# Layer-0 conditioning sums on ScalarE and GpSimd in place of TensorE matvecs

## The chip, the cores and the metric

The kernel runs on one core of one Trainium2 chip. Its time is the device time of one execution in microseconds; the time of a kernel is the median of its runs. All times below are of this metric or of one profiled execution of the kernel before.

## What is computed

The reference is a decoder trunk of two layers over 256 tokens of width 1024, in float32. A vector `c` of 1024 conditions each layer:

```python
c_act = jax.nn.silu(c)
for l in range(DEPTH):
    mod = c_act @ ada_w[l] + ada_b[l]
    sh_m, sc_m, g_m, sh_f, sc_f, g_f = jnp.split(mod, 6, axis=-1)
    h = modulate(rms_norm(x, norm_mix_g[l]), sh_m, sc_m)
    proj = h @ w_in[l]
    ...
    mixed = jnp.concatenate([attn_out, ssm_out], axis=-1) @ w_out[l]
    x = x + g_m[:, None, :] * mixed
    h = modulate(rms_norm(x, norm_ffn_g[l]), sh_f, sc_f)
    ...
    x = x + g_f[:, None, :] * f
```

The mixer between `proj` and `mixed` is a sliding-window attention beside a state-space mixer; `f` is a dense SwiGLU in layer 0 and a top-2-of-8 mixture of experts in layer 1. Each of the six parts of `mod` is a product of a vector of 1024 and a matrix of 1024 x 1024. The change is about two of them in layer 0: the mixer's gate `g_m` and the feed-forward shift `sh_f`.

## The kernel before

All weights come in one fixed order through a stream of 8 raw buffers of 128 x 2080 floats (`Stream`, loads at line 124 on SyncE's queue). A unit is one load of about 1 MB. A buffer is given back when its unit has been read, and the next load in the order waits for a free buffer. Weights for matmuls are split first: ScalarE copies a tile of 128x1024 into a rounded format (`hi`, line 157), VectorE subtracts that from the raw tile (`lo`, line 158), and each product is three matmuls (lines 698 to 700). Splits run about two half units ahead of their use. Conditioning units (kind `raw`) are used as they come, unsplit.

Layer 0 runs so: the first two parts of `mod`; the input projections (features bc and x, then q, kv, z0, z1 in `tok_tile`); beside them the chains of the mixer, small generators that `tick()` advances between matmuls; then `out_proj`, four steps in the order `WO_ORDER`, each with one unit of output weights; then the norm, the modulation, and the dense feed-forward (`ffn`). The framework's scheduler orders the instructions of each engine in advance by a priority that follows the order of tracing; an instruction whose inputs are ready may be moved ahead of one that waits. On the chip each engine then goes through its queue in order.

The parts are numbered relative to the fourth: part -2 is `g_m`, part -1 is `sh_f`, part 0 is `sc_f`, part 1 is `g_f`. Each has four units (`k2` = 0 to 3) of 256 rows of `ada_w`. Parts -2, -1 and 0 are matvecs on TensorE in `ada_half`: for each unit the matmuls at line 610 multiply the column of `c_act`, spread over 32 columns, with the loaded tile, and four column groups add up in one PSUM bank `ps("a")`, of which there is one. After the last unit ScalarE copies the bank (line 615), four transposes (line 618) turn it into columns in the same bank, and VectorE adds the bias (lines 622, 623). The units of part -2 lie among the input projections, one each after x1, q0, q1 and kv (`FILL`, run by `fill()`); those of parts -1 and 0 lie behind the output weights in the stream and behind `out_proj` in the program. Part 1 is not a matvec: `half_late` scales and adds on VectorE into an accumulator and then sums over the partitions with matmuls against ones (line 580).

`g_m` is first needed at the residual update in the last step of `out_proj` (line 1179), `sh_f` and `sc_f` at the modulation after the norm (`make_amp`, `modulate`). GpSimd has little to do: the products of the decay with the state-space scores at line 1043 and one product at line 1060, in each layer, and a few in the router.

Of the kernel before, what the change touches and what calls it, by code (L numbers as in the profile page):

```python
# [7 lines left out]
F32 = mybir.dt.float32  # L8
# [3 lines left out]
AF = mybir.ActivationFunctionType  # L12
OP = mybir.AluOpType
AX = mybir.AxisListType

P = 128
D = 1024
# [202 lines left out]
def trunk(ctx, tc, x, c, positions, ada_w, ada_b, norm_mix_g, norm_ffn_g, w_in, w_out, attn_sinks,  # L220
# [3 lines left out]
    V, A, G, PE = nc.vector, nc.scalar, nc.gpsimd, nc.tensor  # L224
# [4 lines left out]
    act = ctx.enter_context(tc.tile_pool(name="act", bufs=1))  # L229
    psum = ctx.enter_context(tc.tile_pool(name="psum", bufs=1, space=bass.MemoryType.PSUM))  # L230

    def ps(tag):
        return psum.tile([P, 512], F32, name="ps_" + tag, tag=tag, bufs={"w": 3, "m": 3, "d": 1, "a": 1}[tag])
# [6 lines left out]
    def add_w(tag, loads, n):  # L240
        units.append(dict(kind="w", tag=tag, loads=loads, n=n))
# [6 lines left out]
    def add_rows(tag, w2d, r0, nrow):  # L248
        src = w2d[r0:r0 + nrow * P, :].rearrange("(k p) f -> p k f", p=P)
        add_w(tag, [(0, nrow * D, src)], nrow * D)  # L250
# [38 lines left out]
    def add_ada_half(l, part, k2):  # L289
        src = ada_w[l, k2 * 2 * P:(k2 + 1) * 2 * P, 4096 + part * D:4096 + (part + 1) * D].rearrange("(k p) f -> p k f", p=P)  # L290
        units.append(dict(kind="raw", tag=("adah", l, part, k2), n=2048, loads=[(0, 2048, src)]))

    WO_ORDER = (2, 3, 0, 1)

    def wo_units(l):
        for kp in WO_ORDER:
            add_rows(("wo", l), w_out[l], kp * 256, 2)

    def add_first(half, k2):
        rows = ada_w[0, k2 * 2 * P:(k2 + 1) * 2 * P, :]  # L300
        units.append(dict(kind="raw", tag=("first", half, k2), n=2048, loads=[
            (i * D, (i + 1) * D, rows[:, i * D + half * 512:i * D + half * 512 + 512].rearrange("(k p) f -> p k f", p=P))
            for i in range(2)]))

    for k2 in range(4):
        add_first(0, k2)
    FILL = (0, 0, 0, 1, 1, 1, 1, 0, 0)
    n = 0
    win0 = win_units(0)
    for i, j in enumerate(FIRST):  # L310
        win0[j]()
        for k2 in FIRST_FILL.get(i, ()):
            add_first(1, k2)
        for _ in range(FILL[i]):
            add_ada_half(0, -2, n)
            n += 1
    assert n == 4
    wo_units(0)
    for part in (-1, 0):
        for k2 in range(4):  # L320
            add_ada_half(0, part, k2)
    n_ffn = 3 * FFN // 256
    n_late = 3 * KT + 4
    ada_at = [n_late * min(i + 1, LATE_FFN) // LATE_FFN - n_late * min(i, LATE_FFN) // LATE_FFN for i in range(n_ffn)]
    n = 0
# [54 lines left out]
    S = Stream(nc, raw_pool, split_pool, units)  # L380
# [5 lines left out]
    ident = const.tile([P, P], F32)  # L386
# [22 lines left out]
    ones = const.tile([P, P], F32)  # L409
# [21 lines left out]
    ct = const.tile([P, KT], F32)  # L431
    p = ps("w")
# [29 lines left out]
    for b in range(2):  # L462
        for h in range(2):
            p = ps("w")
# [5 lines left out]
    adab = const.tile([P, 96], F32)  # L470
# [47 lines left out]
    modT = [const.tile([P, 48], F32, name=f"modT{l}") for l in range(DEPTH)]  # L518
# [82 lines left out]
    def ada_half(l, part, k2):  # L601
        j, t = S.take_raw(("adah", l, part, k2))
        if k2 == 0:
            ada_ps[0] = ps("a")
        p = ada_ps[0]
        for k in range(2):
            kk = k2 * 2 + k
            for i in range(2):
                q = k * 2 + i
                PE.matmul(p[32 * q:32 * q + 32, :], ct[:, kk:kk + 1].to_broadcast([P, 32]),  # L610
                          t[:, k * D + i * 512:k * D + (i + 1) * 512], start=(k2 == 0), stop=(k2 == 3))
        S.release(j)
        if k2 == 3:
            r = act.tile([P, D], F32, name="adar", tag="adar")[:, 0:512]
            A.activation(r, p, AF.Copy)
            p2 = ps("a")
            for i in range(4):
                PE.transpose(p2[:, i * P:(i + 1) * P], r[:, i * P:(i + 1) * P], ident)
            pv = p2.rearrange("p (j c) -> p c j", j=4)[:, 0:P:32, :]
            o0 = 32 + part * 8  # L620
            dst = modT[l][:, o0:o0 + 8].rearrange("p (c j) -> p c j", c=2)
            V.tensor_tensor(dst, pv[:, 0:2, :], adab[:, l * 48 + o0:l * 48 + o0 + 8].rearrange("p (c j) -> p c j", c=2), op=OP.add)
            V.tensor_tensor(dst, pv[:, 2:4, :], dst, op=OP.add)

    def mod(l, i):
        return modT[l][:, i * 8:(i + 1) * 8]
# [98 lines left out]
    def fill():  # L725
        if filler:
            for f in filler.pop(0):
                f()
# [58 lines left out]
    def mixer(l, h, second=None, third=None):  # L787
# [20 lines left out]
        cbm = cx[:, 0].rearrange("p (i t) -> p i t", i=4)  # L808
# [153 lines left out]
        def wait_for(*keys):  # L962
            while not all(k in ready for k in keys):
                yield 1

        def dt_chain(bx):
# [33 lines left out]
            for ch in range(2):  # L1000
                for g in range(2):
                    spawn(decay(ch, g))
                    yield DEC_Y
# [20 lines left out]
        def decay(ch, g):  # L1024
            bc = ps("m")
            PE.matmul(bc, identb, dmask4.rearrange("p a b -> p (a b)"), start=True, stop=False, skip_group_check=True)
            for h4 in range(4):
                hh = ch * 8 + g * 4 + h4
                PE.matmul(bc[:, h4 * P:(h4 + 1) * P], dta[:, hh:hh + 1].to_broadcast([P, P]), tri, start=False, stop=True,
                          skip_group_check=True)  # L1030
            yield 1
            mt = act.tile([P, 4, P], F32, name="mt", tag="mt" if ch == 0 else "sm", bufs=2 if ch == 0 else 4)
            mts[ch, g] = mt
            for h4 in range(4):
                hh = ch * 8 + g * 4 + h4
                A.activation(mt[:, h4, :], bc[:, h4 * P:(h4 + 1) * P], AF.Exp, bias=nacs[:, hh:hh + 1])
            if ch == 0:
                ec = eac[:, g * 4:g * 4 + 4]
                V.tensor_tensor(ec, bc.rearrange("p (h t) -> p h t", h=4)[:, :, P - 1], acs[:, g * 4:g * 4 + 4], op=OP.subtract)
                A.activation(ec, ec, AF.Exp)  # L1040
            yield from wait_for("cbm")
            yield 1
            G.tensor_tensor(mt, mt, cbm[:, ch * 2 + g, :][:, None, :].to_broadcast([P, 4, P]), op=OP.mult)
            ready.add(("decay", ch, g))

        def x_chain(b0, b1):
# [109 lines left out]
    def out_proj(l, m, norm, route=None):  # L1156
        mhi, mlo, ready = m
        banks = [ps("w"), ps("w"), ps("w"), ps("d")]
        for n, kp in enumerate(WO_ORDER):
            while (("mix", kp) if kp < 2 else ("ssm", kp - 2)) not in ready:  # L1160
                tick()
            if l == 1 and n == 0:
                assert {"y", "k", "qt"} <= ready
                S.lend(first_moe + LIMIT, lambda: [act.tile([P, D], F32, name="slot", tag=t) for t in ("cx", "qr")])
            w = S.take(("wo", l), 2)
            if n == 3 and route:
                route.prepare()
                S.lend(first_moe + LATE_LIMIT, lambda: [act.tile([P, D], F32, name="slot", tag=t) for t in ("misc", "adar")])
                S.lend(first_moe + LIMIT, lambda: [act.tile([P, 2 * D], F32, name="slot", tag="xbc")])
                S.lend(first_moe + SM_LIMIT, lambda: [act.tile([P, 512], F32, name="slot", tag="sm", bufs=4) for _ in range(4)])  # L1170
            for k in range(2):
                kk_ = 2 * kp + k
                last = n == 3 and k == 1
                for m_ in range(8):
                    b = banks[m_ // 2][:, (m_ % 2) * T:(m_ % 2 + 1) * T]
                    mm3(b, w.hi(k, m_ * P, (m_ + 1) * P), w.lo(k, m_ * P, (m_ + 1) * P), mhi[:, kk_, :], mlo[:, kk_, :],
                        n == 0 and k == 0 and m_ % 2 == 0, last)
                    if last:
                        V.scalar_tensor_tensor(xT[:, m_, :], b, mod(l, 2)[:, m_:m_ + 1], xT[:, m_, :], op0=OP.mult, op1=OP.add)
                        norm.add(m_)  # L1180
                        if route:
                            route.add(m_)
                    if m_ == 3:
                        tick()
                S.used()
                tick()
        assert not chains
# [579 lines left out]
        modulate_part(rbc, 0, 0, amps[0], h, range(4, KT))  # L1767


    steps = [lambda k2=k2: ada_half(0, -2, k2) for k2 in range(4)]  # L1770
    for n in FILL:
        filler.append(steps[:n])
        steps = steps[n:]
    m = mixer(0, h, second, third)
    norm = Norm()
    out_proj(0, m, norm)
    for part in (-1, 0):
        for k2 in range(4):
            ada_half(0, part, k2)
    amp = make_amp(0, 1)  # L1780
    h = modulate(norm, 0, 1, amp)
    dn = ffn(h, [lambda k2=k2: half_late(0, 1, k2) for k2 in range(4)] +
# [42 lines left out]
```

## Time and profile before

| what | value |
|---|---|
| median of 3 runs | 1399.41 us (1398.51 to 1399.52) |
| profiled execution, own time | 1397.93 us |
| its span, first to last instruction | 1395.8 us |
| TensorE busy | 1321.7 us (95%) |
| VectorE busy | 857.9 us (61%) |
| ScalarE busy | 643.7 us (46%) |
| GpSimd busy | 20.1 us (1%), 22 instructions |
| mean granted TensorE clock | 0.98 |

The busy shares are of the whole span, over stages with different limits. PE is TensorE's matmuls, PEld its weight loads, DVE VectorE, ACT ScalarE, POOL GpSimd, SP SyncE. The end of a matmul is modelled, so distances from start to start say more than its duration. In rows of a timeline, the bracket at the end is the idle time of the engine before the instruction and what ended it.

### The profile page before, as it was taken

To read this page: it belongs to the slowest core of one execution; us is meant where nothing else is said; L and a number is where in the kernel's file an instruction comes from. 1 tells how busy PE (TensorE), PEld (TensorE's weight loads), DVE (VectorE), ACT (ScalarE), POOL (GpSimd) and SP (SyncE) were. 2 spreads that over 40 slices of the span, in tenths; PEclk is the share of its full clock that TensorE was granted. 3 is DMA by queue.
4 is the path that set the end of the run, shared out by engine and by line. 5 is a ranking of instruction groups with operands and counts; after the bars stand their busy time and mean duration, and the time that the engine had idled before them with its cause. 6 is when DMAs were issued, how large, how long until landed. Compare 5 with 4: busy or idle time off the path is not lost. (4 is left out here: it accounts for less than half of the span.)

```text
span 1395.8 us, 20220 instructions
## 1 busy us (share of the span) xinstructions
PE 1321.7 (95%) x7642; PEld 953.8 (68%) x7642; DVE 857.9 (61%) x1297; ACT 643.7 (46%) x923; POOL 20.1 (1%) x22
## 2 busy tenths in 40 slices
PE   6999999999899979999999999987999999999996
PEld 3788699999798868666464756656557467756643
DVE  5587598778689579556254744546537348845532
ACT  3456454444465547445143543533536236744412
POOL 0020000000020010000000000000000000000000
PEclk9999999999999989999999999997999999999998
DMA  9963799999434549899999999989999999999993
GB/s 324 349 237 109 277 388 363 325 348 340 159 127 146 197 149 340 333 406 400 402 409 409 409 409 409 398 349 400 363 409 409 402 401 409 409 379 409 402 402 127
DMA packets 158214, 468.77 MB, mean 336 GB/s; under 512 B 10560, under 2 KB 39456, under 8 KB 155040
## 3 DMA queue, kind: packets, MB, share of 16 engines
q1 hardware_dynamic: 155616, 466.72, 87.8%
q8 instruction: 61, 1.00, 0.3%
q10 hardware_dynamic: 2496, 0.72, 0.2%
q14 instruction: 41, 0.34, 0.1%
HBM read 466.36 MB, written 1.05 MB: 335 GB/s over the span
## 5 line engine op out<-in xcount | busy, mean ns | idle before, releaser
L158 DVE TENSOR_TENSOR lo<-raw,hi 128x1024 fp32r<-128x1024 f32 (+1 forms) x346 | 413.4, 1226 | 98.5 <-ACT hi L157 95.3
L157 ACT ACTIVATE hi<-raw 128x1024 fp32r<-128x1024 f32 (+1 forms) x346 | 354.9, 1057 | 220.7 <-PE ps_m L699 69.2
L699 PE MATMUL ps_w<-lo,xh 128*128 128x512 f32 x352 | 141.1, 401 | 0.7 <-DVE lo L158 0.7
L700 PE MATMUL ps_w<-hi,xh 128*128 128x512 f32 x352 | 140.3, 400 | 0.2 <-DVE xh L1503 0.2
L698 PE MATMUL ps_w<-hi,xh 128*128 128x512 f32 x352 | 133.8, 404 | 6.9 <-PEq L1246 5.6
L158 DVE TENSOR_TENSOR lo<-slot,hi 128x1024 fp32r<-128x1024 f32 (+1 forms) x112 | 128.0, 1181 | 15.7 <-ACT hi L157 15.7
L157 ACT ACTIVATE hi<-slot 128x1024 fp32r<-128x1024 f32 (+1 forms) x112 | 111.6, 1026 | 33.2 <-PE ps_w L700 25.7
L1673 DVE TENSOR_TENSOR sg<-sg,ps_w 128x512 f32<-128x512 f32 (+1 forms) x32 | 20.9, 654 | 171.6 <-PE ps_w L1524 129.8
L1524 PE MATMUL ps_w<-raw,xl 128*64 128x512 f32 (+1 forms) x624 | 125.7, 545 | 0.0
L698 PE MATMUL ps_m<-act_hi,hi 128*128 128x256 f32 (+1 forms) x368 | 104.6, 285 | 7.6 <-ACT hi L157 4.7
L700 PE MATMUL ps_m<-act_hi,lo 128*128 128x256 f32 (+1 forms) x368 | 104.1, 284 | 0.4 <-DVE lo L158 0.4
L699 PE MATMUL ps_m<-act_lo,hi 128*128 128x256 f32 (+1 forms) x368 | 104.2, 284 | 0.0
L1524 PEld LDWEIGHTS ps_w<-raw,xl 128*64 128x64 f32 x624 | 43.9, 137 | 72.2 <-issue 65.7
L1580 ACT ACTIVATE hh<-ps_m 128x512 fp32r<-128x512 f32 x28 | 16.2, 595 | 154.9 <-PE ps_m L1575 131.8
L698 PEld LDWEIGHTS ps_w<-hi,xh 128*128 128x128 f32 x352 | 67.3, 192 | 23.5 <-issue 5.9
L1524 PE MATMUL ps_w<-slot,xl 128*64 128x512 f32 (+1 forms) x400 | 81.4, 536 | 0.0
L699 PEld LDWEIGHTS ps_w<-lo,xh 128*128 128x128 f32 x352 | 67.4, 191 | 17.7 <-DVE lo L158 1.9
L700 PEld LDWEIGHTS ps_w<-hi,xh 128*128 128x128 f32 x352 | 67.0, 191 | 16.4 <-DVE xh L1503 0.7
L1546 PE MATMUL ps_m<-raw,ht 128*64 128x512 f32 x328 | 76.6, 599 | 0.0
L698 PEld LDWEIGHTS ps_m<-act_hi,hi 128*128 128x128 f32 (+1 forms) x368 | 68.1, 185 | 11.5 <-ACT hi L157 5.2
L1582 DVE TENSOR_TENSOR hl<-ps_m,hh 128x512 fp32r<-128x512 f32 x28 | 18.8, 688 | 92.8 <-ACT hh L1580 92.8
L1672 ACT ACTIVATE sg<-ps_w 128x512 f32<-128x512 f32 (+1 forms) x44 | 24.9, 576 | 102.5 <-PE ps_w L1524 76.6
(428 smaller groups left out, 2484.3 us busy)
## 6 DMA issues: line engine op xcount, KB each, us to landing
raw<-in_moe_w_down SPq DMA_DIRECT2D x84, 1024.0 KB, 13.5
raw<-in_moe_w_gate SPq DMA_DIRECT2D x79, 1024.0 KB, 12.4
raw<-in_moe_w_up SPq DMA_DIRECT2D x61, 1024.0 KB, 12.6
raw<-in_ada_w SPq DMA_DIRECT2D x40, 1024.0 KB, 7.2
slot<-in_moe_w_up SPq DMA_DIRECT2D x25, 1024.0 KB, 14.0
slot<-in_moe_w_gate SPq DMA_DIRECT2D x48, 512.0 KB, 12.7
slot<-in_moe_w_up SPq DMA_DIRECT2D x46, 512.0 KB, 13.8
slot<-in_moe_w_down SPq DMA_DIRECT2D x20, 1024.0 KB, 13.7
```

What stands on the lines that cost most here:

```text
L157: self.last_hi = nc.scalar.activation(hi[:, o:o + w], t, AF.Copy).ins
L158: self.last_lo = nc.vector.tensor_tensor(lo[:, o:o + w], t, hi[:, o:o + w].bitcast(F32), op=OP.subtract).ins
L698: PE.matmul(o_, s_hi, m_hi, start=start, stop=False, skip_group_check=True)
L699: PE.matmul(o_, s_hi, m_lo, start=False, stop=False, skip_group_check=True)
L700: PE.matmul(o_, s_lo, m_hi, start=False, stop=stop, skip_group_check=True)
L1524: PE.matmul(b[half * c_:half * (c_ + 1), 0:wide], xl[:, kk_, :], S.col(j, o_, o_ + wide), start=(kk_ == 0), stop=(kk_ == KT - 1), skip_gro ...
L1546: PE.matmul(y[half * c_:half * (c_ + 1), :], ht[:, ft % nm, ft // nm, :], S.col(j, t_ * D + c_ * 512, t_ * D + (c_ + 1) * 512), start=(ch ...
L1580: A.activation(hh, pv, AF.Copy)
L1582: V.tensor_tensor(hl, pv, hh.bitcast(F32), op=OP.subtract)
L1672: A.activation(s_[:, 0:wide], g_[:, 0:wide], AF.Silu)
L1673: V.tensor_tensor(s_[:, 0:wide], s_[:, 0:wide], u_[:, 0:wide], op=OP.mult)
```

## The change

The matvecs of parts -2 and -1 go. In their place, `slow_half` scales each loaded tile of 128x1024 in its buffer on ScalarE by the matching value of `c_act`, and GpSimd adds the tiles up in the buffer of the part's first unit, which is held until the part is done. The sums after the first product at line 1043 are put behind the latest one that has been traced (`mixed_by`). `slow_out` then adds over the partitions with matmuls against ones, as `half_late` does, and transposes as before. The units come in another order: two units of part -2 after x1 and two after z0, two of part -1 after z1 and one each with the first two output weights. `slow_out` of part -2 stands ahead of the third step of `out_proj`, that of part -1 behind `out_proj`. Part 0 stays a matvec.

```diff
-    FILL = (0, 0, 0, 1, 1, 1, 1, 0, 0)
+    FILL = (0, 0, 0, 2, 0, 0, 0, 2, 2)
+    SLOW = [(part, k2) for part in (-2, -1) for k2 in range(4)]
...
         for _ in range(FILL[i]):
-            add_ada_half(0, -2, n)
+            add_ada_half(0, *SLOW[n])
             n += 1
-    assert n == 4
-    wo_units(0)
-    for part in (-1, 0):
-        for k2 in range(4):
-            add_ada_half(0, part, k2)
+    for i, kp in enumerate(WO_ORDER):
+        add_rows(("wo", 0), w_out[0], kp * 256, 2)
+        if i < 2:
+            add_ada_half(0, *SLOW[n])
+            n += 1
+    assert n == len(SLOW)
+    for k2 in range(4):
+        add_ada_half(0, 0, k2)
...
+    slow_acc = {}
+    mixed_by = []
+
+    def slow_half(l, part, k2):
+        j, t = S.take_raw(("adah", l, part, k2))
+        if k2 == 0:
+            slow_acc[part] = j, t[:, 0:D]
+            A.activation(t[:, 0:D], t[:, 0:D], AF.Copy, scale=ct[:, 0:1])
+        acc = slow_acc[part][1]
+        for k in range(2):
+            kk = k2 * 2 + k
+            if kk:
+                tk = t[:, k * D:(k + 1) * D]
+                A.activation(tk, tk, AF.Copy, scale=ct[:, kk:kk + 1])
+                with ExitStack() as after:
+                    if mixed_by:
+                        after.enter_context(tc.issue_after(mixed_by[-1]))
+                    G.tensor_tensor(acc, acc, tk, op=OP.add)
+        if k2:
+            S.release(j)
+
+    def slow_out(l, part):
+        j, acc = slow_acc.pop(part)
+        p = ps("a")
+        for i in range(2):
+            PE.matmul(p[32 * i:32 * i + 32, :], ones[:, 0:32], acc[:, i * 512:(i + 1) * 512], start=True, stop=True)
+        r = act.tile([P, D], F32, name="adar", tag="adar")
+        A.activation(r[0:64, 0:512], p[0:64, :], AF.Copy)
+        S.release(j)
+        p2 = ps("a")
+        for i in range(4):
+            PE.transpose(p2[:, i * P:i * P + 64], r[0:64, i * P:(i + 1) * P], ident[0:64, 0:64])
...
-            G.tensor_tensor(mt, mt, cbm[:, ch * 2 + g, :][:, None, :].to_broadcast([P, 4, P]), op=OP.mult)
+            mult = G.tensor_tensor(mt, mt, cbm[:, ch * 2 + g, :][:, None, :].to_broadcast([P, 4, P]), op=OP.mult)
+            mixed_by.append(mult.ins)
...
             w = S.take(("wo", l), 2)
+            fill()
+            if l == 0 and n == 2:
+                slow_out(0, -2)
...
-    steps = [lambda k2=k2: ada_half(0, -2, k2) for k2 in range(4)]
-    for n in FILL:
+    steps = [lambda s=s: slow_half(0, *s) for s in SLOW]
+    for n in FILL + (1, 1):
         filler.append(steps[:n])
         steps = steps[n:]
...
     out_proj(0, m, norm)
-    for part in (-1, 0):
-        for k2 in range(4):
-            ada_half(0, part, k2)
+    slow_out(0, -1)
+    for k2 in range(4):
+        ada_half(0, 0, k2)
```

## Rows read from the trace of the kernel before

**Rows 1.** Windows: busy us (instructions) per engine, granted clock, DMA share, GB/s.
```profile
60.00:140.00 80.00, 78.35 (x601) 65.32 (x599) 66.09 (x174) 50.40 (x126) 8.00 (x5) 1.00 0.53 182
166.90:170.50 3.60, 3.55 (x15) 3.25 (x16) 3.60 (x10) 2.08 (x5) 0.00 (x0) 0.54 1.05 403
220.00:260.00 40.00, 40.00 (x338) 39.02 (x337) 31.78 (x26) 17.04 (x20) 0.00 (x0) 1.00 0.99 351
```
**Rows 2.** Timeline of TensorE, layer 0's mixer: start us, us, line, operation.
```profile
66.06 0.50 PE L698 MATMUL ps_w<-hi,act_hi 128*128 128x512 f32 x1
...
95.81 0.63 PE L922 MATMUL ps_m<-ident,qr 128*128 128x128 f32 x4 [0.53 <-DVE qr L829]
96.36 1.06 PE L610 MATMUL ps_a<-raw,ct 128*32 128x512 f32 x8
97.36 0.39 PE L698 MATMUL ps_w<-hi,act_hi 128*128 128x256 f32 x1
...
116.02 0.39 PE L698 MATMUL ps_w<-mx_hi,hi 128*128 128x256 f32 x1
```
**Rows 3.** Timeline of TensorE, layer 1's mixer.
```profile
397.78 1.05 PE L1012 MATMUL ps_m<-xbc 128*128 128x128 f32 x8
...
400.30 0.39 PE L698 MATMUL ps_w<-hi,act_hi 128*128 128x512 f32 x1
...
444.63 0.38 PE L698 MATMUL ps_w<-mx_hi,hi 128*128 128x256 f32 x1
```
**Rows 4.** Timeline of TensorE, from layer 0's norm to the feed-forward.
```profile
159.27 0.50 PE L665 MATMUL ps_m<-sel,npart 128*128 128x1 f32 x4
160.14 3.64 PE L610 MATMUL ps_a<-raw,ct 128*32 128x512 f32 x32 [0.37 <-PE ps_m L665]
...
164.55 0.66 PE L618 MATMUL ps_a<-ident,adar 128*128 128x128 f32 x4
166.93 0.40 PE L698 MATMUL ps_m<-act_hi,hi 128*128 128x256 f32 x1 [1.72 <-ACT act_hi L692]
```
**Rows 5.** Timeline of TensorE, from layer 1's first norm to its projections.
```profile
366.25 0.61 PE L665 MATMUL ps_m<-sel,npart 128*128 128x1 f32 x4 [0.47 <-ACT npart L662]
...
371.66 0.38 PE L698 MATMUL ps_m<-act_hi,hi 128*8 128x256 f32 x1 [1.18 <-ACT act_hi L692]
```
**Rows 6.** Timeline of TensorE, column sum of `half_late`.
```profile
197.46 1.05 PE L580 MATMUL ps_a<-adacc,ones 128*32 128x512 f32 x4
```
**Rows 7.** Groups by line, ScalarE, 60 to 140: count, busy us, mean ns, idle before.
```profile
L157 ACT ACTIVATE hi<-raw 128x1024 fp32r<-128x1024 f32 x18 | 19.1, 1065 | 10.2 <-PE ps_w L700 9.8 <-PE ps_d L699 0.4
```
**Rows 8.** Timeline of GpSimd, layer 0's mixer.
```profile
80.97 1.28 POOL L1043 TENSOR_TENSOR mt<-mt,cx 128x512 f32<-128x512 f32 x1 [79.26 <-ACT mt L1036]
83.03 3.51 POOL L1043 TENSOR_TENSOR mt<-mt,cx 128x512 f32<-128x512 f32 x2 [0.79 <-ACT mt L1036]
86.51 1.04 POOL L1060 TENSOR_TENSOR cx<-xx,eac 128x512 f32<-128x512 f32 x1
87.51 2.27 POOL L1043 TENSOR_TENSOR mt<-mt,cx 128x512 f32<-128x512 f32 x1
```
**Rows 9.** One line's instructions, L1404 on GpSimd: ns min/median/max.
```profile
L1404 POOL TENSOR_TENSOR htok_l<-ht,htok_h x3: 1277/1317/1318, 497.1 to 501.4; 128x512 fp32r<-128x512 f32 x3
```
**Rows 10.** Timeline of VectorE, splits beside GpSimd's products, both layers.
```profile
83.22 2.18 DVE L158 TENSOR_TENSOR lo<-raw,hi 128x1024 fp32r<-128x1024 f32 x1
...
86.66 1.98 DVE L158 TENSOR_TENSOR lo<-raw,hi 128x1024 fp32r<-128x1024 f32 x1
...
416.42 1.48 DVE L158 TENSOR_TENSOR lo<-raw,hi 128x1024 fp32r<-128x1024 f32 x1 [0.53 <-ACT hi L157]
```
**Rows 11.** One line's instructions, L158 (60 to 140) and L829: ns min/median/max.
```profile
L158 DVE TENSOR_TENSOR lo<-raw,hi x18: 1208/1218/2176, 60.6 to 135.1; 128x1024 fp32r<-128x1024 f32 x18
...
L829 DVE TENSOR_TENSOR qr<-rm,rm x4: 679/684/1775, 88.6 to 428.3; 128x512 f32<-128x512 f32 x4
```
**Rows 12.** Timeline of SyncE's queue, loads of parts -1 and 0.
```profile
85.97 50.72 SPq L124 DMA_DIRECT2D raw<-in_ada_w  x8
```

More of the change, by code (lines that the diff above doesn't have):

```diff
@@ L623, in ada_half @@
             V.tensor_tensor(dst, pv[:, 2:4, :], dst, op=OP.add)
+    slow_acc = {}
[28 more added lines that the diff above has]
+            PE.transpose(p2[:, i * P:i * P + 64], r[0:64, i * P:(i + 1) * P], ident[0:64, 0:64])
+        pv = p2.rearrange("p (j c) -> p c j", j=4)[:, 0:64:32, :]
+        o0 = 32 + part * 8
+        V.tensor_tensor(modT[l][:, o0:o0 + 8].rearrange("p (c j) -> p c j", c=2), pv,
+                        adab[:, l * 48 + o0:l * 48 + o0 + 8].rearrange("p (c j) -> p c j", c=2), op=OP.add)
     def mod(l, i):
```

## The prediction

> **What bounds the kernel now.** I read the windows first, to find out what sets the pace where the change acts and whether a shift there survives to the end. In the feed-forward stage TensorE is busy for all 40.00 us of 220 to 260 at full clock, with VectorE at 31.8 and ScalarE at 17.0 [rows 1]. Nothing there can take up a microsecond that is won or lost earlier, and the later stages start from TensorE's progress, so I carry every shift to the end one for one. In layer 0's mixer, from 60 to 140, TensorE is busy for 78.35 of 80 us, but VectorE is busy for 66.09 too and ScalarE for 50.40, while GpSimd has only 8.00 [rows 1]. So this stretch has two engines near their limit, and the question of the whole case is which of the two a microsecond is taken from.
>
> Then TensorE's timeline. One half of a matvec part is 8 matmuls of 128x512 and pushes the next projection matmul back by 1.00 us (96.36 to 97.36) [rows 2]. Layer 1 runs the same mixer without any such matvecs and is the best witness for what taking them out can give. From its first q matmul to its first output-projection matmul it needs 444.63 - 400.30 = 44.33 us, and 1.0 us of small matmuls (line 1012) that layer 0 has inside its stretch lie ahead of it in layer 1: 45.3 us [rows 3]. Layer 0 needs 116.02 - 66.06 = 49.96 us [rows 2]. That is 4.6 us more, of which three halves are 3.0.
>
> After the output projection the chain runs through the norm: from the matmul at line 665 over the reciprocal root on VectorE to the first feed-forward matmul. It takes 166.93 - 159.27 = 7.66 us [rows 4]. Between the two stand 32 matvec matmuls of part 0 (3.64 us from 160.14): they could not start earlier, because part -1 held the single bank `ps_a`, and the amplitude waits for their transposes at 164.55 [rows 4]. The same chain in front of layer 1, with no matvecs, takes 371.66 - 366.25 = 5.41 us [rows 5].
>
> **The change part by part: TensorE.** It loses 8 halves of 1.00 us, 8.0 us in all, and gains two column sums of four matmuls, 1.05 us each by the like sum of the feed-forward shift [rows 6], 2.1 us. The transposes stay. Net that is 5.9 us less work. What reaches the end is asked place by place.
>
> Part -2 lies in the mixer. Layer 1 says that up to 4.6 us can go, if VectorE keeps up; at worst nothing goes, if VectorE sets the pace. I take the four halves, 4.0 us. Its sum moves ahead of the third step of the output projection, where TensorE runs dense: +1.05 us. Together -2.95 (from -4.6 to +1.05).
>
> Part -1 lies around the output projection and in front of the norm. Its sum can now be made during the output projection, so `ps_a` comes free earlier and part 0's matmuls, which stay, go into the places that part -1's had; the reciprocal root is then left alone. The difference between the two chains, 7.66 - 5.41 = 2.25, is the upper bound; nothing is the lower one, if the sums are late. I take -2.0, near layer 1, as its chain is the same code.
>
> **ScalarE** gets 16 scalings of 128x1024. The nearest row is the split's copy of the same size, 1,065 ns [rows 7]: 17 us, against 29.6 us that ScalarE is idle from 60 to 140 [rows 1]. They stand in order among the copies and exponentials that feed VectorE and TensorE. Free would be 0; if one of six delays a waiting unit by its length, about 3. I take +1.0, and the idle time is the cover: without it all 17 would be on the path.
>
> **GpSimd** gets 14 sums of 128x1024, all with both inputs in SBUF. None is in the trace. A sum of half the size takes 1.04 us at least (line 1060, with one input broadcast) [rows 8] and 1.317 with two full inputs (line 1404) [rows 9]. Doubled, this gives 2.1 to 2.6 us; I take 2.5, near the full inputs, so 35 us (29 to 37). GpSimd has the time. VectorE hasn't: when GpSimd works on SBUF, a VectorE instruction with two SBUF inputs stands still. The split at line 158 takes 1.21 us at its least, and 2.18 and 1.98 beside GpSimd's products; line 829 takes 0.68 and once 1.77 [rows 8, 10, 11]. In turn the products at 83.03 and 87.51 stretch (3.51 for two, 2.27 for one, against 1.28 alone): the two engines take turns [rows 8]. So layer 0's five GpSimd instructions, 4 x 1.28 + 1.04 = 6.2 us of work, cost VectorE 0.97 + 0.77 + 1.09 = 2.8 us, a share of 0.46. In layer 1 the same five cost only 1.48 - 1.21 = 0.27 [rows 10, 11], a share of 0.04. These are my bounds, 1.5 to 17 us. I take 0.4, so 14 us: the new sums stand in layer 0, they are twice as long, so that a VectorE instruction that meets one waits longer, and VectorE splits a weight tile there 18 times in 80 us [rows 11].
>
> How much of the 14 reaches TensorE? VectorE is idle for 80 - 66.09 = 13.9 us in the stretch [rows 1], so at best nothing; at worst all of it. After the 2.8 us above, TensorE waited for VectorE only 0.53 us (line 922 at 95.81) [rows 2], a share of 0.19: one short burst fits into the lead that the splits have. A burden that lasts through the whole attention doesn't, because that idle time is largely time in which VectorE waits for products of the other engines, and it moves along when they are late. I let 5 of the 14 be absorbed: +9.0 (from 0 to +17).
>
> A sentence of the Trainium skill gives another price: "GPSIMD Engine Reference", section 3.1, measures a GpSimd add of 2,048 elements at 4,497 ns, so half of it, 2.25 us, is an estimate for one sum here. By that page 14 sums take 31.5 us, 12.6 of them as VectorE's waiting and 7.6 on the path, and the total below would be 1.4 us lower. The trace has no sum of this length. The same page's section 4.1 advises VectorE for elementwise work, since GpSimd is about half as fast; no row here weighs that for this size.
>
> **Loads.** The eight units of parts -2 and -1 are issued among the projections' and output weights, and SyncE's queue is passed in order. Before, the last 8 conditioning loads trickle out for 50.72 us from 85.97, because no buffer is free [rows 12]. Afterwards two of eight buffers stay held, each until its sum is read, but the other six are released before the norm. The queue is slack, so I price this at 0; it would cost if an output weight came behind a unit that GpSimd holds.
>
> **Sum** against the profiled execution, 1397.93 us (span 1395.8): -2.95 - 2.0 + 1.0 + 9.0 = +5.05, so 1402.98. The median of the runs is 1.48 above the profiled execution: 1404.5.
>
> **Rivals.**
> (a) GpSimd's sums fall between VectorE's two-input work as in layer 1, a share of 0.04. Then VectorE loses 1.5 us, all absorbed, the scalings cost nothing, and -4.95 is left: 1394.5 as a median; with layer 1's full 4.6 and 2.25, 1393.6 (-6.85 + 1.05). For it: VectorE is idle for 13.9 us of the stretch, and what it does otherwise than with two SBUF inputs isn't held up; against it: layer 0 has shown 0.46. It decides as soon as less than 2.2 us of waiting reaches TensorE. Chance 0.25.
> (b) The two cancel: a share of 0.19 of the 14 us reaches TensorE as at 95.81, 2.7 us, with +1.0 for ScalarE: -1.3, so 1398.2. Chance 0.20.
> (c) GpSimd falls behind: the 11 sums behind the products (the last of which starts at 87.51) run from about 90; if each takes 2.5 us and waits for two splits of 1.21, they end at 144, and with late scalings near 157, when part -1's sum is due for the norm. From there on it decides: the tail gains nothing (+2.0) and the first feed-forward matmul waits for sum, transposes and shift, some 3 us more by the 2.4 us from 164.55 to 166.93: +10, so 1409.5. Against it: their units are loaded early. Chance 0.10.
> (d) The forecast. Chance 0.45.
>
> The waits have a second price. After TensorE stood still for 1.72 us before 166.93, the granted clock was 0.54 from 166.9 to 170.5, its lower level, 1.2 GHz instead of 2.4 [rows 1, 4]; that cost some 1.7 us. One or two more such stops are the upper part of my range.
>
> **Numbers.** About 0.2%, 2.8 us, is what a measurement tells from no change. Faster: (a), 0.25. Same: (b), 0.20. Slower: (c) and (d), 0.55. The forecast's own range is 1401 to 1412 (2.7 more or less of the waiting hidden; a stop of the clock or two more). The range for 8 in 10 takes in (a): 1393 to 1413.
>
> **What would show it.** Right: GpSimd busy some 35 us more; in layer 0's mixer splits of about 2 us where 1.2 is clean, VectorE's busy time 10 us or more above 66; the first output-projection matmul later than 116.02; line 665 to the first feed-forward matmul in 5.4 us. Wrong: splits that stay at 1.2 us beside the sums, or line 698 after the mixer at 112, would give rival (a). What would make me wrong most easily is the order: sums that run while VectorE evicts PSUM.

## The result and the profile after

The changed kernel takes 1416.50 us (median of 5 runs, 1413.38 to 1416.97) against 1398.94 us for the kernel before (median of 5 runs beside it): a ratio of 1.0118 (95% interval 1.0107 to 1.013), 17.6 us slower by the medians. The sign of the forecast holds, its size doesn't: +5.05 was forecast, and the time lies above the range. The profiled execution took 1414.5 us with a span of 1412.7 us, 16.9 more than the span before.

The windows come first, as before the change (columns as in [rows 1]).
```profile
60.00:140.00 80.00, 65.75 (x429) 57.71 (x429) 76.55 (x153) 52.39 (x106) 45.07 (x19) 0.89 0.55 189
180.00:190.00 10.00, 8.88 (x50) 8.56 (x50) 6.31 (x16) 4.46 (x9) 0.00 (x0) 0.66 0.79 291
220.00:260.00 40.00, 40.00 (x341) 40.00 (x340) 32.04 (x25) 17.39 (x19) 0.00 (x0) 1.00 1.02 373
```
In the mixer TensorE is busy for 65.75 of 80 us where it was 78.35, and VectorE for 76.55 where it was 66.09, with fewer instructions (153 for 174). So VectorE now sets the pace. The granted clock fell from 1.00 to 0.89. The feed-forward stage is as dense as before.

TensorE's timeline shows where the time goes; it answers to [rows 2 to 5].
```profile
64.53 0.80 PE L739 MATMUL ps_w<-hi,act_hi 128*128 128x512 f32 x2 [0.22 <-DVE xbc L991]
...
97.95 1.09 PE L963 MATMUL ps_m<-ident,qr 128*128 128x128 f32 x4 [3.73 <-DVE qr L870]
109.22 0.47 PE L884 MATMUL ps_m<-ident,kr 128*128 128x128 f32 x1 [2.96 <-DVE kr L872]
127.41 1.09 PE L1148 MATMUL ps_m<-ident,zy 128*128 128x128 f32 x4 [5.50 <-DVE zy L1142]
...
131.29 0.58 PE L739 MATMUL ps_w<-mx_hi,hi 128*128 128x256 f32 x1
...
172.43 1.47 PE L614 MATMUL ps_a<-raw,ct 128*32 128x512 f32 x9
...
176.72 0.60 PE L706 MATMUL ps_m<-sel,npart 128*128 128x1 f32 x4
...
181.62 0.58 PE L739 MATMUL ps_m<-act_hi,hi 128*128 128x256 f32 x1 [1.12 <-ACT act_hi L733]
```
The first q matmul is 1.53 us earlier (66.06 to 64.53). The first output-projection matmul is 15.27 later (116.02 to 131.29): nearly the whole loss arises between these two. Three waits for VectorE, 12.2 us in all, stand there, where before there was one of 0.53 [rows 2]. The first feed-forward matmul is 14.69 later (166.93 to 181.62), and the end 16.9 later; the clock of 0.66 from 180 to 190, behind the stops at the norm, lies in the last step.

GpSimd's timeline answers to [rows 8].
```profile
57.91 7.35 POOL L646 TENSOR_TENSOR raw<-raw 128x1024 f32<-128x1024 f32 x3 [56.20 <-ACT raw L642]
82.39 1.31 POOL L1084 TENSOR_TENSOR mt<-mt,cx 128x512 f32<-128x512 f32 x1 [17.13 <-ACT mt L1077]
...
91.60 32.07 POOL L646 TENSOR_TENSOR raw<-raw 128x1024 f32<-128x1024 f32 x11
```
Eleven sums run back to back from 91.60 to 123.67, a mean of 2.9 us each. In the same stretch VectorE's timeline reads:
```profile
92.87 2.18 DVE L158 TENSOR_TENSOR lo<-raw,hi 128x1024 fp32r<-128x1024 f32 x1
94.98 2.82 DVE L870 TENSOR_TENSOR qr<-rm,rm 128x512 f32<-128x512 f32 x1
...
101.03 2.44 DVE L872 TENSOR_TENSOR kr<-rm,rm 128x128 f32<-128x128 f32 x1
103.40 3.40 DVE L158 TENSOR_TENSOR lo<-raw,hi 128x1024 fp32r<-128x1024 f32 x1
...
116.04 2.08 DVE L1134 TENSOR_TENSOR zy<-zy 128x512 f32<-128x512 f32 x1
118.05 3.42 DVE L158 TENSOR_TENSOR lo<-raw,hi 128x1024 fp32r<-128x1024 f32 x1
121.39 1.27 DVE L918 TENSOR_REDUCE st<-ps_m 128x2 f32<-128x512 f32 x2
122.59 1.10 DVE L675 TENSOR_SCALAR rs_v<-gs 128x2 f32<-128x2 f32 x1
```
Splits of 1.21 us take up to 3.42, and line 870 takes 2.82 where 0.68 is clean [rows 11]. This instruction makes the `qr` that TensorE waited 3.73 us for. Line 918, which reads PSUM, is not stretched. I added up, over all VectorE instructions from 45 to 200 us, what each took beyond the shortest of its line and operands in any of the traces: 5.6 us before, 24.9 after. This sum is called the excess below.

One line's instructions (ns min/median/max), splits first:
```profile
L158 DVE TENSOR_TENSOR lo<-raw,hi x16: 1214/1440/3424, 64.7 to 137.4; 128x1024 fp32r<-128x1024 f32 x16
...
L642 ACT ACTIVATE raw<-raw,ct x14: 1135/1142/1270, 56.7 to 118.6; 128x1024 f32<-128x1024 f32 x14
```

### The profile page after: what moved, and what is told of

It reads as the page before. It is cut to its first block, busy times and chain, and to the rows that moved or that the text cites. A ratio compares the mean times of both kernels' runs of the same rounds, so it can differ in the third digit from the quotient of the medians.

```text
span 1412.7 us, 20171 instructions
## 1 busy us (share of the span) xinstructions
PE 1324.0 (94%) x7586; PEld 959.4 (68%) x7586; DVE 876.6 (62%) x1295; ACT 659.3 (47%) x939; POOL 59.2 (4%) x36
## 3 DMA queue, kind: packets, MB, share of 16 engines
HBM read 466.36 MB, written 1.05 MB: 331 GB/s over the span
## 5 line engine op out<-in xcount | busy, mean ns | idle before, releaser
L158 DVE TENSOR_TENSOR lo<-raw,hi 128x1024 fp32r<-128x1024 f32 (+1 forms) x346 | 422.3, 1253 | 99.2 <-ACT hi L157 97.5
L158 DVE TENSOR_TENSOR lo<-slot,hi 128x1024 fp32r<-128x1024 f32 (+1 forms) x112 | 128.2, 1184 | 15.6 <-ACT hi L157 15.4
L741 PEld LDWEIGHTS ps_w<-hi,xh 128*128 128x128 f32 x352 | 67.2, 191 | 16.4 <-DVE xh L1548 0.7
```

Of the source, the lines that this page charges most:

```text
L158: self.last_lo = nc.vector.tensor_tensor(lo[:, o:o + w], t, hi[:, o:o + w].bitcast(F32), op=OP.subtract).ins
L741: PE.matmul(o_, s_lo, m_hi, start=False, stop=stop, skip_group_check=True)
```

## The experiments

The theory: GpSimd's sums hold VectorE up, and TensorE waits for VectorE. The rivals: ScalarE's scalings in the order of its queue, the new order of the loads, and GpSimd being late with its own work and with the buffers. Each ratio is to runs of the kernel before on the same chip.

**No sums.**
```diff
-                    G.tensor_tensor(acc, acc, tk, op=OP.add)
```


> The changed kernel without GpSimd's 14 sums; ScalarE's 16 scalings, the order of the loads and both column sums stay (the sums themselves are left out, so each part keeps only its first scaled row block). Theory (the sums keep VectorE's two-input instructions waiting, and that is the loss): VectorE's splits are back at 1.2 us, first output-projection matmul at 113 to 117 us instead of 131.29, and the time falls from 1416.5 to 1393 to 1399 us. Rival, ScalarE's 17 us of scalings in the order of its queue are the loss: still above 1408 us. Rival, the new order of the loads is the loss: still above 1408 us, though buffers come free sooner here.

1398.80 us, ratio 1.0000 (0.9991 to 1.0009). The splits of this run, by one line's instructions:
```profile
L158 DVE TENSOR_TENSOR lo<-raw,hi x19: 1207/1219/2295, 64.2 to 136.8; 128x1024 fp32r<-128x1024 f32 x19
```
Median 1,219 ns again, and the output projection starts at 116.23. Neither scalings nor order are the loss: without the sums the time is that of the kernel before. But nothing is gained either: the 4 us that the removed matvecs were to bring are missing, which two runs below follow up.

**No scalings.**
```diff
-                A.activation(tk, tk, AF.Copy, scale=ct[:, kk:kk + 1])
```


> The changed kernel without ScalarE's 16 scalings; GpSimd sums the tiles as loaded (the factors of c are left out). Theory: the 14 sums stay, so the time stays at 1412 to 1417 us; the scalings are worth 0 to 3 us. Sums that needn't wait for a scaling can start earlier, so the stretch of long VectorE instructions moves forward. Rival, ScalarE's scalings are the loss: 1405 us or less.

1416.22 us, 1.0125 (1.011 to 1.0141): the loss without any scaling. The splits' median is 2.06 us here:
```profile
L158 DVE TENSOR_TENSOR lo<-raw,hi x15: 1210/2059/3425, 68.1 to 137.5; 128x1024 fp32r<-128x1024 f32 x15
```

**The order alone.** All eight halves by `ada_half`, at the changed kernel's places; no `slow_out`.
```diff
-    steps = [lambda s=s: slow_half(0, *s) for s in SLOW]
+    steps = [lambda s=s: ada_half(0, *s) for s in SLOW]
```


> TensorE's matvecs as before, but at the places and in the order of loads of the changed kernel: both parts' eight halves in the input-projection's slots and ahead of the first two output-projection steps, no scaling, no sum, no column sum. Theory: the order alone costs nothing; part -1's four halves leave the stretch behind the last output-projection step (-0.6 to -2.8 us by the two traces) and go into stretches in which TensorE partly waits, so 1395 to 1400 us. Rival, the order of the loads (input and output projection weights held up behind the eight halves) is the loss: above 1408 us.

1402.41 us, 1.0025 (1.0016 to 1.0034): 3.3 us slower, above what the theory gave and far below its rival. The first output-projection matmul is 5.73 us later than before, as part -1's matvecs now stand in the mixer, and only 1.5 come back by the first feed-forward matmul.

**Writing in place of summing.** One write of zeros for each sum, then three.
```diff
-                    G.tensor_tensor(acc, acc, tk, op=OP.add)
+                    for _ in range(3):   # or once
+                        G.memset(tk, 0.0)
```


> In place of each of the 14 sums GpSimd writes zeros over the scaled tile (128x1024, nothing read), at the same place in its queue, with the same waits, and the buffers are released behind it (the sums are left out). Theory (a GpSimd instruction that reads holds up VectorE's two-input instructions): splits of 1.2 us, 1393 to 1400 us, even if GpSimd is busy for 20 us or more with the writing. Rival, what GpSimd's queue delays (its own products behind the sums, the buffers that it releases late): if one write takes over 2 us the time stays above 1408 us. Rival, any GpSimd instruction on the memory holds VectorE up: above 1405 us, with splits of 2 us.

> Three writes of zeros in place of each of the 14 sums (42 instructions that read nothing, at 0.95 us as the run with one write showed, so about 40 us of GpSimd instead of the sums' 36 us), with the same waits and the buffers released behind the third. Theory (what holds VectorE up is the sums' reading): splits of 1.2 us, 1396 to 1401 us. Rival, GpSimd's length of work (its products behind the sums, buffers released late) is the loss: 1408 us or more, as with the sums.

One write each (0.95 us): 1398.68 us, 1.0000 (0.999 to 1.0009), as the theory has it. Three each: 1413.34 us, 1.010 (1.0083 to 1.0117), the rival's time. The theory's expectation fell, but VectorE's timeline of that run shows another cause than the rival's:
```profile
110.02 1.22 DVE L158 TENSOR_TENSOR lo<-raw,hi 128x1024 fp32r<-128x1024 f32 x1
111.46 1.29 DVE L919 TENSOR_REDUCE st<-ps_m 128x2 f32<-128x512 f32 x2 [0.22 <-PE ps_m L903]
112.78 10.02 DVE L676 TENSOR_SCALAR rs_v<-gs 128x2 f32<-128x2 f32 x1
112.86 9.95 DVE L677 TENSOR_SCALAR rs_v<-gs 128x2 f32<-128x2 f32 x1
```
and GpSimd's and TensorE's timelines of the same run:
```profile
94.98 29.80 POOL L647 MEMSET raw<- 128x1024 f32 x33
```
```profile
128.10 0.45 PE L1149 MATMUL ps_m<-ident,zy 128*128 128x128 f32 x1 [11.89 <-DVE zy L1143]
```
The splits stay at 1.22 us beside the writes: these two-input instructions are not held up by one that only writes. But two tiny `TENSOR_SCALAR` on two elements per partition, started 0.08 us apart, wait 10 us together, through ten writes in a row, and one wait of TensorE, 11.89 us, is most of the loss. So it is VectorE again and not GpSimd's lateness, since TensorE waits for `zy` of VectorE; but reading is not the only thing that holds VectorE up. The Trainium skill, "SBUF — State Buffer", section "Who interferes with whom", has both halves: two inputs contend with GpSimd's reads and not with its writes, and a `tensor_scalar` may take the shared ports with its two-port mode. It says that the other engine is blocked for one whole instruction; the 10.02 us over ten writes of 0.95 are more than that.

**One operand.** GpSimd multiplies the tile by one in place.
```diff
-                    G.tensor_tensor(acc, acc, tk, op=OP.add)
+                    G.tensor_scalar(tk, tk, 1.0, None, op0=OP.mult)
```


> In place of each of the 14 sums GpSimd multiplies the scaled tile by one in place: one operand read instead of two, 128x1024 (the sums are left out). If a single reading operand is enough to hold VectorE's two-input instructions up, they stretch again and the loss goes with GpSimd's busy time: 14 instructions of 1 to 2.5 us, half of it lost, 1405 to 1416 us. If only GpSimd instructions with two operands from the memory do it: splits of 1.2 us and 1396 to 1401 us.

1403.96 us, 1.0031 (1.0013 to 1.0048), between the two expectations. GpSimd is busy for 41.0 us with these 14, no less than with sums. One line's instructions, the splits:
```profile
L158 DVE TENSOR_TENSOR lo<-raw,hi x17: 1208/1221/2301, 65.1 to 134.9; 128x1024 fp32r<-128x1024 f32 x17
```
Their median is 1,221 ns: of eight that run beside these instructions, six take 1.21 to 1.23 us and two take 1.71 and 2.06, where all five beside the eleven sums took 2.18 to 3.42. The excess is 13.4, 8.0 more than without sums, and 5.6 of that lie in small instructions of 0.55 to 1.00 us instead of 0.15 to 0.21. So one reading operand holds VectorE up, but less, and mostly other instructions. What decides which VectorE instruction is held is not settled by this run.

**Sums cut into four.**
```diff
-                    G.tensor_tensor(acc, acc, tk, op=OP.add)
+                    for c0 in range(0, D, 256):
+                        G.tensor_tensor(acc[:, c0:c0 + 256], acc[:, c0:c0 + 256], tk[:, c0:c0 + 256], op=OP.add)
```


> Each sum cut into four of 128x256 (56 instructions of about 0.65 to 0.8 us, the same bytes). Theory A (a VectorE instruction waits for the whole GpSimd instruction that is running, then has its turn): a wait of up to 0.8 us instead of up to 2.7 us for each, so VectorE's excess falls from about 19 us to 6 to 10 us and the time to 1404 to 1411 us. Theory B (the two engines share by the element, the length of one instruction doesn't matter): 1413 to 1418 us. GpSimd's own sums then take longer in all, 40 to 50 us.

1416.28 us, 1.0129 (1.0107 to 1.0152): theory B's time. One line's instructions:
```profile
L647 POOL TENSOR_TENSOR raw<-raw x56: 716/741/1740, 60.6 to 132.0; 128x256 f32<-128x256 f32 x56
```
Each wait is shorter, as in theory A (a small instruction takes at most 0.76 us), but the sums take 49.0 us instead of 38.7 and meet more instructions: 30 are held by more than 0.3 us, instead of 16. The excess is 19.8, far above theory A's 6 to 10; TensorE waits 9.1 us once, for `zy`. Neither theory is shown whole.

**VectorE does it all**, by `scalar_tensor_tensor`. The expectation errs on one point: the first row blocks were still scaled by ScalarE, so nothing was left out.
```diff
-                A.activation(tk, tk, AF.Copy, scale=ct[:, kk:kk + 1])
...
-                    G.tensor_tensor(acc, acc, tk, op=OP.add)
+                V.scalar_tensor_tensor(acc, tk, ct[:, kk:kk + 1], acc, op0=OP.mult, op1=OP.add)
```


> No ScalarE scaling and no GpSimd sum: VectorE multiplies and adds in one instruction per row block, 14 of 128x1024 at about 1.28 us by the same form behind the feed-forward (the two first row blocks stay unscaled, so two factors of c are left out), about 18 us of VectorE at the same places. Theory (VectorE sets the pace of layer 0's mixer, and any of its microseconds there reaches TensorE): nearly all 18 us arrive, less up to 5 us, 1410 to 1417 us, about what the sums on GpSimd cost. Rival, VectorE has room and it was only the blocking by GpSimd: 1398 to 1404 us.

1404.75 us, 1.0044 (1.0028 to 1.0061), under the theory's 1410 and just above the rival's 1404. By groups of instructions:
```profile
L642 DVE SCALAR_TENSOR_TENSOR raw<-raw,ct 128x1024 f32<-128x1024 f32 x14 | 17.9, 1279 | 1.0 <-ACT raw L636 1.0
```
VectorE pays 17.9 us of its own work. The run is 5.6 us slower than the kernel before on its chip; the run with nothing in the matvecs' place in the same order (below) is 2.1 us faster on its own. So 7.8 us of the 17.9 arrive: VectorE had room for more than half. By the same measure the changed kernel's scalings and sums cost 17.6 + 2.1 = 19.7 us. Handing the work to the idle engine cost about two and a half times as much as giving it to the busy one.

**Half of it.** Part -2 alone, then part -1 alone by `slow_half`, the other by `ada_half`.
```diff
+    steps = [lambda s=s: (slow_half if s[0] == -2 else ada_half)(0, *s) for s in SLOW]   # or -1
```


> Only part -2 (the gate) by ScalarE and GpSimd, 7 sums; part -1 by TensorE's matvecs, in the changed kernel's order of loads. From 1402.4 us with both parts on TensorE in this order to 1416.5 us with both on GpSimd. Theory (each sum beside VectorE's two-input instructions costs about 1.2 us): 7 sums give 7 to 10 us, 1407 to 1412 us. Rival (one long GpSimd queue is what does it, and half of it is harmless): 1399 to 1404 us.

> Only part -1 (the shift) by ScalarE and GpSimd, 7 sums; part -2 by TensorE's matvecs, in the changed kernel's order of loads. These are the sums that come latest, beside the last of the mixer's VectorE work. Theory: 7 to 10 us above 1402.4 us if they still meet VectorE's two-input instructions, 1407 to 1412 us; GpSimd's busy time is halved to 17 to 19 us. Rival as for the other half: 1399 to 1404 us.

Part -2: 1404.50 us, 1.0039 (1.0025 to 1.0052); part -1: 1408.73, 1.0067 (1.0049 to 1.0085). Over the order alone (1402.41) that is 2.1 and 6.3 us, with the gain from the matvecs that go already taken off. The first missed its expectation: three of its sums run from 58.77, ahead of the mixer's tight part, by GpSimd's timeline:
```profile
58.77 7.35 POOL L646 TENSOR_TENSOR raw<-raw 128x1024 f32<-128x1024 f32 x3 [57.06 <-ACT raw L642]
...
92.40 11.70 POOL L646 TENSOR_TENSOR raw<-raw 128x1024 f32<-128x1024 f32 x4
```
Both together cost 14.1 over the order alone, more than 2.1 and 6.3. The excess itself adds up: 6.7 and 11.3 us more than with the order alone, 18.1 for both. TensorE's waits between the first q matmul and the first output-projection matmul don't: 4.1 and 5.1 us more, 12.4 for both. Nor does the loss of clock: 0.96 and 0.98 over 60 to 140, 0.89 for both. So with half the sums VectorE catches up more of what it is held up; with all of them less.

**Part -1 only, meant to be late.** Order and matvecs of part -2 as before; `slow_half` of part -1 stands behind `out_proj` in the program.
```diff
     out_proj(0, m, norm)
+    for k2 in range(4):
+        slow_half(0, -1, k2)
     slow_out(0, -1)
```


> Order and matvecs of the kernel before, but part -1 (the shift) by ScalarE's scalings and 7 GpSimd sums placed behind the output projection's steps, beside a VectorE that is busy for 8 to 13 of 20 us instead of for nearly all. Theory (a sum costs only where VectorE's two-input instructions are on the path): 1396 to 1401 us, with sums of about 2.3 us. Rival (the sums themselves, or the wait for the last of them, cost wherever they stand): 7 sums of 2.5 us in a row behind the last load end after the norm is ready, 1403 to 1412 us, with TensorE waiting at the column sum.

1409.24 us, 1.0069 (1.0054 to 1.0084). It didn't test what it was to: GpSimd's timeline has the sums in the mixer, as soon as the loads are there.
```profile
102.07 2.36 POOL L644 TENSOR_TENSOR raw<-raw 128x1024 f32<-128x1024 f32 x1 [10.63 <-ACT raw L640]
107.85 13.41 POOL L644 TENSOR_TENSOR raw<-raw 128x1024 f32<-128x1024 f32 x5 [3.42 <-issue]
128.22 2.39 POOL L644 TENSOR_TENSOR raw<-raw 128x1024 f32<-128x1024 f32 x1 [6.96 <-ACT raw L640]
```
Place in the program is no place in time on an engine with nothing else to do. As a run it shows that seven sums, with their scalings and in place of part -1's matvecs, cost 10 us.

**Part -1 really late**, behind a copy of one element of the mixer's output, by GpSimd, then by VectorE.
```diff
+            if l == 0 and n == 2:
+                mixed_by.append(G.tensor_copy(gate, mhi[:, 1, 0:1].bitcast(F32)).ins)   # or V
             w = S.take(("wo", l), 2)
```


> Part -2 by matvecs and in the order of before; part -1 by ScalarE's scalings and 7 sums that GpSimd starts only behind a one-element copy of the mixer's output that the third output-projection step reads, so at about 138 us, when VectorE's waits no longer hold TensorE up. Theory (a sum costs where VectorE's two-input instructions are on TensorE's path, and little elsewhere): 1396 to 1402 us, against 1409.2 when the 7 sums ran at 102 to 130 us. Rival, the sums cost by their number wherever they stand: 1405 to 1411 us; rival, they end too late for the norm: TensorE waits at the column sum, past 160 us.

> As the run before this one, but part -1 multiplied and added by VectorE (8 instructions of 128x1024, 0.7 to 1.3 us each, about 9 us), also behind the mixer's output of the third step; no scaling, no GpSimd. VectorE is busy for 8 of 20 us in that stretch before, so 1396 to 1400 us, a gain of at most 2 us (22 matvecs of 0.13 us off, a column sum of 1.05 us on). Rival, VectorE's 9 us stand ahead of the residual and norm work: 1401 to 1406 us.

On GpSimd: 1410.15 us, 1.0068 (1.0055 to 1.0082). Its timeline and TensorE's:
```profile
142.03 18.26 POOL L643 TENSOR_TENSOR raw<-raw 128x1024 f32<-128x1024 f32 x7
```
```profile
160.35 1.92 PE L651 MATMUL ps_a<-raw,ones 128*32 128x512 f32 x2 [8.54 <-POOL raw L643]
```
The second rival came true: the mixer is hardly disturbed (first output-projection matmul at 117.83), and seven sums end at 160.29, too late by 8.54 us. The time alone would fit the first rival too; the wait decides. So on GpSimd neither of the two places is good: in the mixer they hold VectorE, behind it they are the wait themselves. Whether all sums could run ahead of the mixer's tight part, as three of part -2's do, was not tried. On VectorE: 1399.79 us, 0.9999 (0.9986 to 1.0012), no change; its eight instructions fit into that stretch.

**Nothing in place of the matvecs**, in the old and in the new order: no matvecs of parts -1 and -2, no scalings, no sums; the column sums stay.
```diff
-                A.activation(tk, tk, AF.Copy, scale=ct[:, kk:kk + 1])
...
-                    G.tensor_tensor(acc, acc, tk, op=OP.add)
```


> The kernel before with its order of loads, but without the matvecs of both parts and with nothing in their place (no scaling, no sum; two column sums of a bare row block stay): the ceiling of any version that takes these matvecs off TensorE. The prediction counted 4.0 us for part -2 and 2.0 us for part -1, less 1.05 us for a column sum, so 1393 to 1395.5 us against 1399. If TensorE would wait anyway for what the matvecs fill (the loss outside the sums lies in this term), 1397 to 1399.5 us.

> The same in the changed kernel's order of loads: neither scalings nor sums nor matvecs. If the order of loads is what ate the gain (4 us outside the sums), this stays at 1398 to 1399.5 us while the run in the old order is at 1395 or less. If ScalarE's scalings ate it, this falls to 1394 to 1396 us, 3 to 4 us below the run that had scalings and no sums (1398.8).

Old order: 1395.87 us, 0.9967 (0.9955 to 0.9979), that is -4.1, a little above the 1393 to 1395.5 expected. By the spans it is -1.9 (1395.8 to 1393.9), as the kernel before was profiled in an execution 2 us below its median on this chip (1397.93 against 1399.97). New order: 1397.85 us, 0.9987 (0.9978 to 0.9996), -2.1. The intervals touch, so the 2 us between them are likely rather than certain; the traces agree: the first q matmul comes 1.84 us earlier in the new order, but the stretch from it to the output projection takes 51.73 us instead of 48.00. The place of part -2's column sum differs between the two as well. The table of TensorE's waits (us in total, times, longest) has this line in the new order, which the old one hasn't:
```profile
PE ps_w L733 <- DVE rm L859: 2.5, 1, 2.5
```
VectorE's timeline has two splits just ahead of this `rm`, beside GpSimd's own products (80.91 to 89.82), 4.21 us where 2.4 is clean:
```profile
83.26 4.21 DVE L158 TENSOR_TENSOR lo<-raw,hi 128x1024 fp32r<-128x1024 f32 x2
```
So in the new order too GpSimd holds VectorE at a place where TensorE waits for it; the excess is 6.7 us there and 3.6 in the old order. In these two orders no version with these column sums can be expected to gain more than the first, about 0.3%, and it leaves the work out. None of the runs that do the whole work beats the kernel before.

## Why the forecast had the sign and missed the size

The forecast's sum against the runs, as medians:

| step | forecast | measured | from |
|---|---|---|---|
| matvecs off TensorE, column sums on | -4.95 | -4.1 | nothing in their place, old order |
| order of the loads | 0 | +2.0 | new order against old |
| 16 scalings | +1.0 | +1.9 | no sums against new order |
| 14 sums | +9.0 | +17.8 | changed kernel against no sums |
| sum | +5.05 | +17.6 | |

The lines come from several chips; about 1 us of each is uncertain.

**The step that failed** is the price of GpSimd's sums, +9.0: a share of 0.4 of 35 us, 5 of them absorbed, and nothing in the sum for the clock. The mechanism is as forecast: GpSimd's sums hold VectorE's two-input instructions, TensorE waits. The sizes were too small. The sums were busy for 38.7 us, since GpSimd is held by VectorE in turn: they take 2.37 us at the least and 3.34 at the most, and in the run with part -1 behind the mixer's output 2.34 to 2.39 while VectorE stood idle. The excess was 24.9 - 5.4 (no sums) = 19.5 us, a share of 0.50; 0.46 had been the larger witness [rows 8, 10, 11], and I had stepped back from it. From the first q matmul to the first output-projection matmul TensorE waits 14.25 us, without the sums 1.84: 12.4 of the 19.5 reached it and 7 were absorbed. That is the part that the forecast had let be absorbed, 5 of 14, though no row had given it; there the forecast was lucky.

What GpSimd holds up was put too simply as well. Beside writes, and mostly beside one-operand reads, the splits stay at 1.2 us; and of what VectorE does otherwise than with two inputs, which rival (a) took to be free, a `TENSOR_SCALAR` of 128x2 took 1.10 us beside the sums and 10.02 beside the writes, where 0.16 is clean.

**The clock** was named as a second price, for the upper part of the range, and left out of the sum. It is the other missing part. Around and after the three long waits the granted clock is at its lower level, 1.2 GHz instead of 2.4 (windows of the changed kernel, columns as in [rows 1]):
```profile
95.60:102.43 6.83, 4.48 (x22) 4.51 (x22) 6.83 (x7) 3.35 (x5) 6.75 (x3) 0.50 0.48 157
109.25:112.67 3.42, 3.42 (x16) 3.42 (x17) 3.41 (x3) 0.77 (x2) 3.34 (x2) 0.50 1.04 399
126.32:133.15 6.83, 5.74 (x22) 4.03 (x23) 6.26 (x22) 4.08 (x13) 0.00 (x0) 0.50 0.71 257
```
TensorE is busy for 13.64 us in these. Its timeline has matmuls of 128x256 in the second window and just behind it, back at full clock:
```profile
109.92 0.41 PE L741 MATMUL ps_w<-hi,act_lo 128*128 128x256 f32 x1
110.13 0.41 PE L739 MATMUL ps_w<-hi,act_hi 128*128 128x256 f32 x1
...
113.04 0.28 PE L739 MATMUL ps_w<-hi,act_hi 128*128 128x256 f32 x1
113.16 0.28 PE L740 MATMUL ps_w<-lo,act_hi 128*128 128x256 f32 x1
```
They start 0.21 us apart, then 0.12. By that these windows cost some 6 us, an estimate. Without the sums the granted clock was 0.97 over the same stretch of 51.68 us, some 1.5 us; so 4 to 5 us come with the sums. With the 12.4 of waits that is about 17, and 16.4 arrived by the spans (1412.7 - 1396.3). No run changes the clock alone, so the two are told apart by these rows only.

**Part -2 and part -1.** The bound from layer 1 was sound as a sum, -4.1 for -4.95. The forecast had counted two column sums of 1.05 us and put only one into its sum; with both it is -3.9. From the norm matmul to the feed-forward it now takes 181.62 - 176.72 = 4.90 us (5.4 forecast, 7.66 before). But from the first output-projection matmul to the norm it takes 45.43 instead of 43.25, since part 0's 32 matvecs now stand ahead of the norm, from 172.43, and no longer in its shadow. Net 0.6 of the 2.0 is left there, with six of the two column sums' eight matmuls inside and the lower clock up to 133.15.

**The new order of the loads**, priced at 0, likely costs some 2 us: not through an output weight behind a held unit, which I had named, but in the projections of the mixer, by the wait for `rm` above.

**ScalarE**: 1,142 ns a scaling, against 1,065 assumed; the size is about right. Beside the sums, leaving the scalings out changed nothing that is clear of noise (17.2 us over the kernel before instead of 17.6).

**Rivals.** (a), a share of 0.04, is refuted by the splits of up to 3.42 us, and (b), 2.7 us at TensorE, by its waits of 12.2. (c) had the sums end at 144 or later; they ended at 123.67, so GpSimd didn't fall behind, though the time is nearer to (c)'s than to mine. Of the signs that were named, GpSimd's busy time (45.07, 37.1 above 8.00), VectorE's (76.55, 10.5 above 66.09), the long splits (seven of 16 took 1.99 us or more; the median is 1.44) and the late output projection all came.

## What to carry to other kernels

Before handing work to an idle GpSimd, count the instructions of VectorE that will run beside it, and price its busy time at half a microsecond of VectorE each; where VectorE had little slack, two thirds of that reached TensorE here, and the stops lowered its clock on top. VectorE doing the same work itself cost two fifths of the price. A long row of such instructions was worse than its parts, since less of it was caught up; cutting them into four didn't help. And first run the kernel with the work simply left out: here that ceiling was 0.3%, and no version that did the work came near it.

## What the runs showed of the hardware

- Eleven GpSimd sums of 128x1024 in a row made VectorE's `TENSOR_TENSOR` of 128x128 take 2.44 us: a small instruction waits as long as a large one. Cutting the sums into 128x256 raised GpSimd's busy time from 38.7 to 49.0 us.
- Forty-two GpSimd writes left the splits at 1.22 us, and two `TENSOR_SCALAR` of 128x2 waited 10.02 and 9.95 us, over ten writes without a turn between. Beside GpSimd's sums, where two-input instructions got a turn each time, the longest excess was 2.2 us (3.42 against 1.21).
- GpSimd instructions of 128x1024 that read one operand took 2.76 us at the least, the sums with two 2.37, and the writes 0.94; six of eight splits beside the one-operand ones were not held (1.21 to 1.23 us).
